# A third seven-product pair in the second half of an up-projection, with three small edits to the order around it

## The chip, the cores and the metric

The kernel runs on one core of a Trainium2 chip. The metric is device time in microseconds of one execution, as the median of the runs given; the profile is one execution of its own, with its own time. The engines are named as in the profile: PE is the matrix engine (PEld its weight loads), DVE the vector engine, ACT the scalar engine, POOL the GpSimd engine, SP the engine whose queue issues most transfers.

## The reference, cut to what matters

One layer of a streaming encoder on 512 positions of width 1024, all in float32. The part that the change touches is the last one, the channel mixer and what follows it:

```python
h = rms_norm(x, norm_ffn_g)
up = causal_dwconv(h @ w_up, conv_ffn_w)      # 1024 -> 2 x 2816, three taps over positions
a, b = jnp.split(up, 2, axis=-1)
x = x + (jax.nn.silu(a) * b) @ w_down         # 2816 -> 1024
return rms_norm(x, norm_f_g)
```

Before it stand a combined input projection, a short gated convolution, an attention with forget gates, and a gated merge of both; the change leaves them alone.

## The kernel before, in words

**Layout.** Features lie on the 128 partitions, the 512 positions in the free dimension. The 2816 hidden features are 22 pairs of blocks: pair `j` is the 128 columns of `a` (`up{2j}`) and the 128 of `b` (`up{2j+1}`).

**Precision.** Each float32 operand is split in a high part of a reduced type and the rest (`wh`, `wl` for weights, `x1h`, `x1l` and `gh`, `gl` for activations), and a product is three matmuls: high by high, rest by high, high by rest. A matmul is 128x128 weights by 256 positions. The split of a weight chunk is one ACT copy (line 275, writes `wh`) and one DVE subtraction (line 279, writes `wl`). `wh` and `wl` have two buffers each, so a chunk's `wh` can be written only when PE has done its last matmul with the `wh` of the chunk two before it, and likewise for `wl`.

**Plain and seven-product work.** A plain up block (`block`) multiplies eight weight blocks by two halves of the positions, three matmuls each: 48 matmuls, 96 a pair. A seven-product step (`seven`, a Strassen scheme) takes a 2x2 set of blocks and computes its eight products as seven. Its weights come in two chunks: `P`, three of the seven products with weights as they are, and `F`, four with sums of weights. A full step holds two such sets (a chunk `P` is 768 columns wide and gives 18 matmuls, a chunk `F` 1024 columns and 24), a half step one (9 and 12). A pair done in two full steps is 84 matmuls. Within a chunk the matmuls with `wh` come first (12 of 18, 16 of 24), those with `wl` after them. The sums of weights are made ahead of time in DRAM by `make_forms`: for each group of steps three transfers of SP and three accumulating transfers of POOL, put off to numbered slots. The sums of the activations are held in `gh` and `gl`: for the down projection six of the seven forms of a pair of pairs are in `go` and one in `ge`; for the up projection the forms of `x1` come through the tiles `y10` to `y13`, one after the other through one buffer: each is fetched from DRAM, split by ACT (`gh<-y`) and DVE (`gl<-y`), and only then is the next fetched.

**Order.** The hidden pairs are in two phases, 0 to 11 and 12 to 21. Each phase runs its up pairs (`up`) and then its part of the down projection as seven-product steps (`STEPS[0]`, `STEPS[1]`, through `seven`); the last products are plain (`dp` chunks). A step is named by its number: chunks `P30`, `F30` belong to step 30. A double like `((2, 6), (2, 7))` stands for outputs of set 2 and hidden pairs of pairs 6 and 7. Which up pairs are in seven products is in `SUP`.

**What the other engines do beside PE.** The result of an up block is multiplied by a row of norms (DVE, line 1171, `fz`), taken through the three taps (`taps`: ACT line 566, DVE lines 567 and 570, `fu`), gated (`glu`: ACT line 1231, POOL lines 1236 and 1243), and every second pair made into forms (DVE lines 1253 to 1258, then `hl` at lines 1262 and 1263). A pair in seven products has more to merge first (`merge`, lines 1192 to 1214). A list `later` holds such work; at each split of a chunk, `run_later` takes from its head what fits a budget in microseconds for that kind of chunk ("u" 1.7, "P" 1.6, "F" 0.75), and stops at a head that is due but too long. `flush` forces what the next matmuls need. Every engine then works through its own rows in the order in which the built program has them, and waits where a row's input isn't there.

**Banks.** PSUM has eight banks. A plain block takes the next in the list `acc`, a seven-product step a set of four: banks 2 to 5 for the pairs in `SUP[1]`, and the same four for set 2 at the end of phase 0, whose values are taken up by `combine` (lines 1282 to 1301).

Of the kernel before, what the change touches and what calls it, by code (L numbers as in the profile page):

```python
# [42 lines left out]
PHASES = ((0, 12), (12, NP))  # L43
# [4 lines left out]
STEPS = (  # L48
    tuple(((i, q), (i, q + 1)) for i, q in ((0, 0), (0, 2), (1, 0), (1, 2), (0, 4), (1, 4)))
    + tuple(((i, q), (i, q + 1)) for i in (3, 2) for q in (0, 2, 4)),  # L50
    (((2, 6), (2, 7)), ((2, 8), (2, 9)), ((0, 6), (0, 7)), ((0, 8), (2, 10)), ((0, 9), (0, 10)))
    + (((1, 6),), ((1, 7), (1, 8)), ((1, 9), (1, 10))),
)

# [3 lines left out]
PLAIN = [(m, k) for m in (6, 7) for k in range(*PHASES[1])]  # L58
PCUTS = (0, 8, 12, 20)

SUP = ((1, 2, 5), (14, 16))
XF = (26, 0)
UPD = tuple(tuple(((j, q), (j, q + 1)) for j in js for q in (0, 2)) for js in SUP)
DOUBLES = GATES + UPD[0] + STEPS[0] + UPD[1] + STEPS[1]
# [6 lines left out]
def block_kernel(ctx, tc, xT, vecs, wv, win, wmix, wo, wup, wst, wdp, outT):  # L71
# [84 lines left out]
    later = []  # L156
    held = dict.fromkeys(NRAW, 0)

    def after_split():

        st = ExitStack()
        for ins in order.values():
            st.enter_context(tc.issue_after(ins))
        return st
# [82 lines left out]
    def flush_only(tags):  # L247

        while n := [n for n, w in enumerate(later) if set(w[2]) & set(tags)]:
            with after_split():  # L250
                later.pop(n[0])[3]()
# [200 lines left out]
    for kb in range(KB):  # L452
        x = xs[kb]
# [236 lines left out]
    z, e, o = (ap.tile([n, S], F32, tag="pp", name=nm, bufs=NPP) for nm in ("fz", "fe", "fo"))  # L690
# [56 lines left out]
    acc, bank_s, bank_t = ring(2, 0, 1), ring(3, 4), ring(5, 6)  # L747
# [26 lines left out]
    for q in (0, 2):  # L774
        f, g = x_sums(slice(q, q + 2))
# [8 lines left out]
    for idx in late:  # L784
        kind, i = divmod(idx, 4)
# [338 lines left out]
    def turns(*ids):  # L1124
        st = list(ids)

        def f(name):
            f.last = st.pop(0)
            flush((f.last,))
            return bank(f.last, name)  # L1130

        return f
# [8 lines left out]
    def up(j, ph, rb2, pu=None):  # L1141
        uu = []

        def tap(i, z):
            u = fp.tile([P, S], F32, tag="fu", name=f"fu{j}{i}", bufs=3)
            taps(u, z, CF + 3 * (2 * j + i))
            uu.append(u)

        if j in SUP[ph]:
            c = 2 * SUP[ph].index(j)  # L1150
            slot()
            seven(
                UPD[ph][c : c + 2], NU[ph] + c, {j: USETS[j]}, lambda q, g: up_form(ph, q, g), of="x",
                done=lambda i, banks, ids: merge(ph, j, banks, ids, rb2, tap, uu),
            )
            slot()
            return
        evacs = []
        for i in range(2):
            slot()  # L1160
            p = pu[i] if pu else block(f"up{2 * j + i}", x1h, x1l, True)
            if i and j + 1 == PHASES[ph][1]:
                split_next()
                if any(("e",) in w[2] for w in later):
                    flush_only((("e",),))
                    split()
            z = [None]

            def mul(i=i, p=p, z=z):
                z[0] = fp.tile([P, S], F32, tag="fz", name=f"fz{j}{i}", bufs=4)  # L1170
                nc.vector.tensor_mul(z[0], p, rb2)

            evac = [(0.7, mul), (1.4, lambda i=i, z=z: tap(i, z[0]))]
            if i:
                evac.append((0, lambda: glu(ph, j, uu)))
            if any(("e",) in w[2] for w in later):
                later.extend((0, us, (("e",), acc.last) if x == 0 else (("e",),), f) for x, (us, f) in enumerate(evac))
            else:
                for _, f in evac:
                    f()  # L1180
# [46 lines left out]
    def glu(ph, j, uu):  # L1227
        a, b = uu
        q, k = j // 2, len(parts) - 1
        g0 = place(ph, q)  # L1230
        nc.scalar.activation(a, a, AF.Silu)
        if j == NP - 1:
            nc.scalar.activation(tbl, a[: 4 * H, :1], AF.Sqrt, scale=0.0, bias=eps[: 4 * H])
        if j % 2 == 0:
            ge = glu.even = fp.tile([P, 2, 2 * P], F32, tag="ge", name=f"ge{q}", bufs=2)
            keep(nc.gpsimd.tensor_mul(ge, a.rearrange(halves_of, h=2), b.rearrange(halves_of, h=2)))  # L1236
            return
        flush_only([("q", x) for x in range(q)])
        ge = glu.even
        go = fp.tile([P, 6, 2 * P], F32, tag="gr", name=f"go{q}")  # L1240

        def mul(eng):
            return eng.tensor_mul(go[:, 0:2, :], a.rearrange(halves_of, h=2), b.rearrange(halves_of, h=2))

        if j + 1 < PHASES[ph][1]:
            keep(mul(nc.gpsimd))
        else:
            later.append((k + 3, 0.7, (("q", q),), lambda: mul(nc.vector)))
        b11, b12 = ge[:, 0, :], ge[:, 1, :]
        b21, b22, t1, t2, t3, t4 = (go[:, i, :] for i in range(6))  # L1250

        def t13():
            nc.vector.tensor_sub(t1, b11, b12)
            nc.vector.tensor_sub(t3, b22, b12)

        def t24():
            nc.vector.scalar_tensor_tensor(t2, t1, -1.0, b22, op0=ALU.mult, op1=ALU.subtract)
            nc.vector.scalar_tensor_tensor(t4, t2, -1.0, b21, op0=ALU.mult, op1=ALU.subtract)

        def hl(src, gs):  # L1260
            def f():
                nc.scalar.activation(gh[:, gs, :], src, AF.Copy)
                nc.vector.tensor_sub(gl[:, gs, :], src, gh.bitcast(F32)[:, gs, :])

            return f


        d = (2, 3, 4) if j + 1 < PHASES[ph][1] else (4, 5, 6)
        w = [(d[0], 0.85, t13), (d[0], 0.85, t24), (d[1], 0.7, hl(ge[:, : 1 + ph, :], slice(g0, g0 + 1 + NF * ph, NF)))]
        w += [(d[x > 0 and 2 or 1], 0.7, hl(go[:, x : x + 2, :], slice(g0 + 1 + x, g0 + 3 + x))) for x in (0, 4, 2)]  # L1270
        at = next((x for x, i in enumerate(later) if ("e",) in i[2]), len(later))
        later[at:at] = [(k + n, us, (("q", q),), f) for n, us, f in w]

# [48 lines left out]
    X, Y = (6, 7, 0, 1), (2, 3, 4, 5)  # L1322
    for ph, (j0, j1) in enumerate(PHASES):
        if ph:
            acc = turns(*(6, 7, 0, 1) * 4)
            make_forms(ND[1], len(DOUBLES), ph)
        for j in range(j0, j1):
            pu = None
            if j == 0:
                nrm = {}  # L1330

                def mid():
                    nrm["c"] = rstd_col([ssq2], NT, 6, "n2")

                def late():
                    nrm["b"] = rstd_sb(rstd_bc(nrm["c"], NT, 7, "n2"), "n2")

                pu = lead(["up0", "up1"], x1h, x1l, mid, late)
            up(j, ph, nrm["b"], pu)
        if not ph:  # L1340
            up_forms(0, 1)
        flush_only((("e",),))
        seven(
            STEPS[ph], ND[ph], ({0: X, 1: Y, 3: X, 2: Y}, {0: X, 1: Y, 2: Y})[ph],
            lambda q, g: (gh[:, place(ph, q) + g, :], gl[:, place(ph, q) + g, :]),
            done=lambda i, banks, ids: combine(ph, i, banks, ids), tick=True,
        )
        assert not todo_bg
# [188 lines left out]
```

## Time and profile before

| | |
|---|---|
| median of 3 runs | 694.79 us (694.62 to 695.16) |
| the profiled execution | 694.18 us, its span 692.4 us |
| PE busy | 683.1 us, 99% of the span |
| DVE busy | 554.2 us, 80% |
| ACT busy | 368.3 us, 53% |
| POOL busy | 190.5 us, 28% |
| up pairs of phase 1 | 523.8 to 631.1 us in the span |
| down steps of phase 1 | 631.1 to 667.8 us |

PE's busy time counts matmuls that overlap in its pipeline as one stretch. In a timeline a row gives the start, the length, the engine, line and operation, and in brackets how long the engine had been idle and what ended that.

### The profile page before, as it was taken

The numbers are of one execution on the slowest core, as the hardware profiler recorded it, in microseconds if no ns is written. First come the engines' busy times: TensorE is split into PE (matmuls) and PEld (weight loads), VectorE is DVE, ScalarE is ACT, GpSimd is POOL, SyncE is SP. The second block draws the span as 40 slices with busy tenths as digits, with TensorE's granted clock in tenths as the row PEclk, the third lists the DMA queues.
The fourth block names the chain that finished last, engine by engine and source line by source line (L and its number), as shares of the span: only waits on it lengthen the run. The fifth ranks groups of instructions, "written<-read, shape, count | busy, mean of one in ns | idle before, by whom it ended". The sixth has DMA issues, their size and how long they took to land. (4 is left out here: it accounts for less than half of the span.)

```text
span 692.4 us, 14690 instructions
## 1 busy us (share of the span) xinstructions
PE 683.1 (99%) x5936; PEld 680.6 (98%) x5936; DVE 554.2 (80%) x858; ACT 368.3 (53%) x579; POOL 190.5 (28%) x201
## 2 busy tenths in 40 slices
PE   9999999999999999999999999999999999999996
PEld 9999999999999999999999999999999999999995
DVE  6677787877578778769879699998787899988894
ACT  5675755554554444546554555545444544545572
POOL 6134947542020201214400144340100325231000
PEclk9999999999999999999999999999999999999998
DMA  8629999552568586788998498888945996676413
GB/s 308 225 67 293 216 243 204 134 120 92 185 144 221 166 268 205 230 308 213 158 313 241 126 233 222 200 242 231 252 149 167 337 231 157 188 168 182 154 31 122
DMA packets 65012, 137.53 MB, mean 199 GB/s; under 512 B 5760, under 2 KB 30352, under 8 KB 64688
## 3 DMA queue, kind: packets, MB, share of 16 engines
q1 hardware_dynamic: 44664, 107.28, 47.2%
q0 software_dynamic: 18464, 26.03, 23.4%
q10 hardware_dynamic: 1816, 3.29, 1.3%
q8 instruction: 46, 0.75, 0.4%
q14 instruction: 22, 0.18, 0.1%
HBM read 132.31 MB, written 47.71 MB: 260 GB/s over the span
## 5 line engine op out<-in xcount | busy, mean ns | idle before, releaser
L211 POOL DMA_DIRECT2D f<-in_wst_dram x66 | 77.7, 1371 | 27.1 <-DMA f<-f 26.8
L309 PE MATMUL p_up<-x1h,wh_up 128*128 128x256 f32 x416 | 81.2, 276 | 0.0
L309 PE MATMUL p_up<-x1l,wh_up 128*128 128x256 f32 x416 | 81.0, 276 | 0.0
L309 PE MATMUL p_up<-x1h,wl_up 128*128 128x256 f32 x416 | 81.0, 276 | 0.0
L279 DVE TENSOR_TENSOR wl_F<-raw_F,wh_F 128x1024 fp32r<-128x1024 f32 (+1 forms) x42 | 55.9, 1330 | 20.0 <-ACT wh_F L275 20.0
L275 ACT ACTIVATE wh_F<-raw_F 128x1024 fp32r<-128x1024 f32 (+1 forms) x42 | 44.3, 1054 | 39.5 <-PE dn L327 28.7
L309 PEld LDWEIGHTS p_up<-x1h,wh_up 128*128 128x128 f32 x416 | 62.7, 188 | 0.0
L309 PEld LDWEIGHTS p_up<-x1l,wh_up 128*128 128x128 f32 x416 | 62.7, 188 | 0.0
L309 PEld LDWEIGHTS p_up<-x1h,wl_up 128*128 128x128 f32 x416 | 62.6, 188 | 0.0
L309 PE MATMUL p_in<-xgh,wh_in 128*128 128x256 f32 x288 | 56.8, 279 | 0.0
L309 PE MATMUL p_in<-xgh,wl_in 128*128 128x256 f32 x288 | 56.6, 278 | 0.0
L309 PE MATMUL p_in<-xgl,wh_in 128*128 128x256 f32 x288 | 56.5, 278 | 0.0
L279 DVE TENSOR_TENSOR wl_P<-raw_P,wh_P 128x768 fp32r<-128x768 f32 (+1 forms) x42 | 41.7, 992 | 14.7 <-ACT wh_P L275 8.6
L327 PE MATMUL dn<-gh,wh_F 128*128 128x256 f32 x216 | 51.2, 277 | 1.2 <-ACT wh_F L275 1.2
L275 ACT ACTIVATE wh_P<-raw_P 128x768 fp32r<-128x768 f32 (+1 forms) x42 | 35.1, 835 | 32.1 <-PE dn L327 23.2
L327 PE MATMUL dn<-gl,wh_F 128*128 128x256 f32 x216 | 51.0, 276 | 0.0
L1236 POOL TENSOR_TENSOR ge<-fu,fu 128x512 f32<-128x512 f32 x11 | 20.1, 1831 | 110.5 <-DVE fu L570 85.6
L279 DVE TENSOR_TENSOR wl_up<-raw_up,wh_up 128x1024 fp32r<-128x1024 f32 x34 | 43.8, 1288 | 7.4 <-ACT wh_up L275 7.4
L275 ACT ACTIVATE wh_up<-raw_up 128x1024 fp32r<-128x1024 f32 x34 | 35.8, 1054 | 19.4 <-PE p_up L309 9.3
L309 PEld LDWEIGHTS p_in<-xgh,wh_in 128*128 128x128 f32 x288 | 44.7, 188 | 0.7
L309 PEld LDWEIGHTS p_in<-xgl,wh_in 128*128 128x128 f32 x288 | 43.7, 188 | 0.0
L309 PEld LDWEIGHTS p_in<-xgh,wl_in 128*128 128x128 f32 x288 | 43.6, 188 | 0.0
(343 smaller groups left out, 2211.8 us busy)
## 6 DMA issues: line engine op xcount, KB each, us to landing
raw_F<-f SPq DMA_DIRECT2D x41, 512.0 KB, 5.7
raw_up<-in_wup_dram SPq DMA_DIRECT2D x34, 512.0 KB, 5.6
raw_P<-in_wst_dram SPq DMA_DIRECT2D x41, 384.0 KB, 5.4
raw_in<-in_win_dram SPq DMA_DIRECT2D x24, 512.0 KB, 3.6
f<-in_wst_dram POOLq DMA_DIRECT2D x41, 256.0 KB, 6.8
f<-in_wst_dram SPq DMA_DIRECT2D x20, 512.0 KB, 7.1
f<-in_wst_dram POOLq DMA_DIRECT2D x20, 512.0 KB, 9.1
f<-f SPq DMA_DIRECT2D x40, 256.0 KB, 6.5
```

Of the source, the lines that this page charges most:

```text
L211: return lambda: keep(nc.gpsimd.dma_start(dst, src, accum_op=ALU.add))
L275: ins = nc.scalar.activation(hi, raw, AF.Copy)
L279: ins = nc.vector.tensor_sub(lo, raw, hi.bitcast(F32))
L309: keep(nc.tensor.matmul(out[:, cs], w, x[:, cs], start=start and i == 0 and c == 0, stop=stop and i == 2 and c == len(cut) - 1,))
L327: keep(nc.tensor.matmul(out, wl if x == 1 else wh, xl if x == 2 else xh, start=opens and bk not in seen, stop=closes and bk not in left,))
L1236: keep(nc.gpsimd.tensor_mul(ge, a.rearrange(halves_of, h=2), b.rearrange(halves_of, h=2)))
```

## The change

```diff
-    (((2, 6), (2, 7)), ((2, 8), (2, 9)), ((0, 6), (0, 7)), ((0, 8), (2, 10)), ((0, 9), (0, 10)))
+    (((2, 6), (2, 7)), ((2, 8), (2, 9)), ((0, 6), (0, 7)), ((0, 8),), ((2, 10),), ((0, 9), (0, 10)))
     + (((1, 6),), ((1, 7), (1, 8)), ((1, 9), (1, 10))),
...
-SUP = ((1, 2, 5), (14, 16))
+SUP = ((1, 2, 5), (13, 15, 17))
...
             if i and j + 1 == PHASES[ph][1]:
                 split_next()
-                if any(("e",) in w[2] for w in later):
-                    flush_only((("e",),))
-                    split()
+                split()
+                flush_only((("e",),))
...
+            elif i and j + 1 == PHASES[ph][1]:
+                with after_split():
+                    for _, f in evac:
+                        f()
             else:
                 for _, f in evac:
                     f()
...
-        w += [(d[x > 0 and 2 or 1], 0.7, hl(go[:, x : x + 2, :], slice(g0 + 1 + x, g0 + 3 + x))) for x in (0, 4, 2)]
+        w.append((d[2], 1.7, hl(go, slice(g0 + 1, g0 + 7))))
...
-            acc = turns(*(6, 7, 0, 1) * 4)
+            acc = turns(*(6, 7, 0, 1) * 3, 6, 7)
```

**Pairs.** In phase 1 pairs 13, 15 and 17 are in seven products, where 14 and 16 were: three pairs for two. They use the same four banks 2 to 5 as before, the plain blocks the other four in turn. The steps of phase 1's down projection get higher numbers (36 to 44 for 34 to 41). The weight sums of the third pair, `f34`, are a third group, made in phase 0 behind the two that were there.

**A down step divided.** The step of `(0, 8)` and `(2, 10)` becomes two half steps, 39 and 40, with the same products; phase 1's down steps have six groups of weight sums where they had five.

**The six gated forms.** `go` was split into `gh` and `gl` in three pieces of 512 columns, two of them due a chunk apart, at 0.7 us each in the budget; now it is one piece of 1536 columns, due at the later time and 1.7 us in the budget.

**The last evacuation.** At the end of each phase the last up block's taps and gate stood right behind its matmuls; now both chunks of the first down step are split first.

What the built programs show of this at three places follows. The first is the start of phase 1, on DVE; `xm` there is the residual that `combine` adds set 2 of phase 0 to, from bank tile `dn1823`. Before:

```order
L279 TENSOR_TENSOR wl_up26_7050<-raw_up26_6808,wh_up26_7049 128x1024
L567 SCALAR_TENSOR_TENSOR fu120_6969<-fz120_6967,vec_64,fu120_6969 128x511
L1079 TENSOR_TENSOR gl_3989<-y13_6877,gh_3988 128x1024
L570 SCALAR_TENSOR_TENSOR fu120_6969<-fz120_6967,vec_64,fu120_6969 128x510
L1294 TENSOR_TENSOR xm_2605<-xm_2605,dn1823_6730 128x512
```

After, DVE again, at the same place:

```order
L279 TENSOR_TENSOR wl_P30_7034<-raw_P30_6791,wh_P30_7033 128x768
L567 SCALAR_TENSOR_TENSOR fu120_6957<-fz120_6955,vec_64,fu120_6957 128x511
L1079 TENSOR_TENSOR gl_3989<-y13_6864,gh_3988 128x1024
L570 SCALAR_TENSOR_TENSOR fu120_6957<-fz120_6955,vec_64,fu120_6957 128x510
L1297 TENSOR_TENSOR xm_2605<-xm_2605,dn1823_6712 128x512
```

The rows are the same but for the chunk; PE's chunk behind pair 12 was `up26`, a plain block in banks 0 and 1, and is now `P30`, whose fifth matmul writes the bank that held `dn1823`:

```order
L327 MATMUL dn30134_7041<-x1h_3990,wh_P30_7033 128x256
L327 MATMUL dn30134_7041<-x1l_3991,wh_P30_7033 128x256
L327 MATMUL dn30132_7039<-x1h_3990,wh_P30_7033 128x256
L327 MATMUL dn30132_7039<-x1l_3991,wh_P30_7033 128x256
L327 MATMUL dn30133_7040<-gh_3988,wh_P30_7033 128x256
```

The second place is the change from up to down in phase 1, on ACT. `fu210` and `fu211` are the last pair's taps, `tbl` the use of a newly loaded function table. Before:

```order
L275 ACTIVATE wh_P34_8267<-raw_P34_8063 128x768
L566 ACTIVATE fu210_8197<-fz210_8195,vec_64 128x512
L1231 ACTIVATE fu210_8197<-fu210_8197 128x512
L1233 ACT_TABLE_LOAD
L1233 ACTIVATE tbl_73<-fu210_8197,ex_87 32x1
L275 ACTIVATE wh_F34_8304<-raw_F34_8065 128x1024
L566 ACTIVATE fu211_8273<-fz211_8271,vec_64 128x512
L275 ACTIVATE wh_P35_8334<-raw_P35_8134 128x768
```

After:

```order
L275 ACTIVATE wh_P36_8242<-raw_P36_8023 128x768
L566 ACTIVATE fu210_8185<-fz210_8183,vec_64 128x512
L275 ACTIVATE wh_F36_8252<-raw_F36_8025 128x1024
L1265 ACTIVATE gh_3988<-ge9_7968 128x2x256
L1234 ACTIVATE fu210_8185<-fu210_8185 128x512
L1265 ACTIVATE gh_3988<-go9_8108 128x1536
L1236 ACT_TABLE_LOAD
L1236 ACTIVATE tbl_73<-fu210_8185,ex_87 32x1
L566 ACTIVATE fu211_8260<-fz211_8258,vec_64 128x512
L275 ACTIVATE wh_P37_8318<-raw_P37_8091 128x768
```

The gate and the table load moved from ahead of the first `F` chunk to ahead of the second `P` chunk, and the forms of `ge9` and `go9` stand there too. The same move at the end of phase 0 puts the gate of pair 11 (`fu110`) behind the first `F` chunk, without a table load.

The third place is the divided step, on ACT. Before:

```order
L1262 ACTIVATE gh_3988<-ge10_8131 128x2x256
L275 ACTIVATE wh_P37_8453<-raw_P37_8263 128x768
L1262 ACTIVATE gh_3988<-go10_8279 128x512 x3
L275 ACTIVATE wh_F37_8483<-raw_F37_8265 128x1024
L275 ACTIVATE wh_P38_8513<-raw_P38_8302 128x768
```

After:

```order
L275 ACTIVATE wh_P39_8433<-raw_P39_8238 128x384
L1265 ACTIVATE gh_3988<-ge10_8181 128x2x256
L275 ACTIVATE wh_F39_8452<-raw_F39_8240 128x512
L275 ACTIVATE wh_P40_8470<-raw_P40_8250 128x384
L1265 ACTIVATE gh_3988<-go10_8268 128x1536
L275 ACTIVATE wh_F40_8487<-raw_F40_8316 128x512
```

The forms `go10` stood behind the split of the chunk whose matmuls begin with `(0, 8)`; they now stand behind that of `P40`, the half step that begins with `(2, 10)` itself. DVE has the subtractions `gl` in the same places.

## The prediction

> **What bounds the kernel now.** I read the page first, then PE's waits, then PE's timeline where those waits fall, then the ACT and DVE rows around the three places that the change moves.
>
> ```profile
> span 692.4 us, 14690 instructions
> PE 683.1 (99%) x5936; PEld 680.6 (98%) x5936; DVE 554.2 (80%) x858; ACT 368.3 (53%) x579; POOL 190.5 (28%) x201
> PEclk9999999999999999999999999999999999999998
> ```
>
> PE is busy from end to end at full clock. So the time is PE's matmuls plus what PE waits, and a change is worth matmuls saved plus waits saved, less waits made. PE's waits in the part that changes:
>
> ```profile
> PE dn L327 <- ACT wh_F L275: 1.2, 2, 0.7
> PE dn L327 <- DVE wl_F L279: 0.4, 1, 0.4
> PE p_up L327 <- DVE wl_up L279: 0.2, 1, 0.2
> ```
>
> Four waits, all for a chunk's split. PE's timeline gives the matmul's pace and each wait's place:
>
> ```profile
> 320.00 0.39 PE L309 MATMUL p_wo<-ml,wh_wo 128*128 128x256 f32 x2
> ...
> 337.00 0.39 PE L309 MATMUL p_wo<-ml,wh_wo 128*128 128x256 f32 x2
> ...
> 468.62 0.38 PE L327 MATMUL dn<-gh,wh_F 128*128 128x256 f32 x1 [0.66 <-ACT wh_F L275]
> ...
> 535.16 0.28 PE L327 MATMUL p_up<-x1h,wh_up 128*128 128x256 f32 x1
> ...
> 554.09 0.28 PE L327 MATMUL dn<-gl,wh_F 128*128 128x256 f32 x1
> 554.72 0.38 PE L327 MATMUL dn<-x1h,wl_F 128*128 128x256 f32 x1 [0.35 <-DVE wl_F L279]
> 554.94 0.51 PE L327 MATMUL dn<-gh,wl_F 128*128 128x256 f32 x3
> ...
> 610.02 0.73 PE L327 MATMUL p_up<-x1h,wl_up 128*128 128x256 f32 x4 [0.15 <-DVE wl_up L279]
> ...
> 633.78 0.38 PE L327 MATMUL dn<-gh,wh_F 128*128 128x256 f32 x1 [0.50 <-ACT wh_F L275]
> ...
> 650.00 1.07 PE L327 MATMUL dn<-gh,wl_F 128*128 128x256 f32 x8
> ```
>
> From 320.00 to 337.00 are 75 such rows of two: 17.00/150 = 0.1133 us a matmul. That makes a plain block 5.44 us, a chunk P 2.04 (wh until 1.36), a chunk F 2.72 (wh until 1.81), halves of these in a half step. A wait costs more than its bracket: at 554.09 the next start was due at 554.20, came at 554.72, and the one behind it took 0.22 instead of 0.11, so 0.63 is lost for a bracket of 0.35. I take bracket plus 0.28 everywhere: 0.94, 0.63, 0.43 and 0.78, together 2.78 us.
>
> **The change, part by part.**
>
> *One more seven-product pair* removes 96 - 84 = 12 matmuls: 12 x 0.1133 = -1.36 us, all on the path. The third pair brings 3584 columns of splits where 2048 were, and a merge, to DVE, which has this room in the stretch of phase 1's up pairs:
>
> ```profile
> 523.80:631.10 107.30, 106.79 (x939) 106.40 (x938) 93.10 (x133) 53.19 (x74) 32.86 (x24) 1.00 0.78 215
> ```
>
> DVE (third busy time) has 14 us free of 107. The extra split is 1.23 x 1536/1024 = 1.8 us by the row of 1024 columns below, the merge some 2.7 us, so it fits on the whole; placing decides. Following DVE's new order row by row at the measured lengths, each wl lands 1 to 3 us before its use behind pair 13, also where 554.72 and 610.02 waited, since the forms' rows now stand elsewhere: -0.63 and -0.43. Were they to wait again, these return. The six more accumulating transfers of POOL and the three more groups of weight sums run beside this; they are due tens of microseconds before their chunk, and I cost them at nothing; if SP's queue, where later raw loads stand behind them, runs late, PE waits for raw weights, which no row of before shows.
>
> *Start of phase 1.* This is new. The rows of ACT and DVE:
>
> ```profile
> 533.00 1.06 ACT L1076 ACTIVATE gh<-y 128x1024 fp32r<-128x1024 f32 x1 [1.73 <-DMA y<-ys]
> 536.08 0.63 ACT L1231 ACTIVATE fu<-fu 128x512 f32<-128x512 f32 x1 [2.01 <-DVE fu L570]
> 536.62 1.05 ACT L275 ACTIVATE wh_up<-raw_up 128x1024 fp32r<-128x1024 f32 x1
> ...
> 534.10 1.23 DVE L1079 TENSOR_TENSOR gl<-y,gh 128x1024 fp32r<-128x1024 f32 x1 [1.46 <-ACT gh L1076]
> 535.24 0.74 DVE L570 SCALAR_TENSOR_TENSOR fu<-fz,vec,fu 128x510 f32<-128x510 f32 x1
> 535.90 0.68 DVE L1294 TENSOR_TENSOR xm<-xm,dn 128x512 f32<-128x512 f32 x1
> ...
> 541.36 1.76 DVE L279 TENSOR_TENSOR wl_P<-raw_P,wh_P 128x768 fp32r<-128x768 f32 x1
> ```
>
> The transfer of y13 lands at 533.00; behind it in DVE's queue stand gl, fu120 and line 1294, which empties its bank at 536.58. Before, nobody on PE needed that. Now the chunk in this place is P30, and its fifth matmul, due at 535.16, writes that bank: 536.58 + 0.05 - 535.16 = 1.47, and 0.11 for the restart: +1.6 us. (F30's wh, in the place of 536.62, is ready at 537.7, and F30 is due at 538.35 then; without the bank wait it would wait itself, 537.7 - 536.75 = 1.0.) P31's wl follows 0.6 us before 541.36, and in its 1.76 us, where such a row is 0.95 in quiet, ends at 542.5, about 0.1 after its use: +0.2. Together +1.8; bounds 1.0 and, if y13 lands 1 us later, 2.8.
>
> *The last evacuation.* In phase 0 F18's wh no longer stands behind the gate: it can start 0.20 after its buffer is free (650.00 against ACT's 650.20 below) and takes 1.05, while P18 takes 2.04: the wait at 468.62 goes, -0.94. P19's wh behind it has 3.4 us and is in time. In phase 1 the wait at 633.78 goes as well, -0.78, but what stood ahead of F is now ahead of the next P:
>
> ```profile
> 630.54 0.63 ACT L1231 ACTIVATE fu<-fu 128x512 f32<-128x512 f32 x1 [2.15 <-DVE fu L570]
> 631.19 1.28 ACT L1233 ACT_TABLE_LOAD   x1
> ...
> 632.69 1.04 ACT L275 ACTIVATE wh_F<-raw_F 128x1024 fp32r<-128x1024 f32 x1
> 633.64 0.71 ACT L566 ACTIVATE fu<-fz,vec 128x512 f32<-128x512 f32 x1
> 634.25 0.83 ACT L275 ACTIVATE wh_P<-raw_P 128x768 fp32r<-128x768 f32 x1
> ...
> 641.65 0.61 ACT L1262 ACTIVATE gh<-ge 128x512 fp32r<-128x512 f32 x1
> ...
> 650.20 1.07 ACT L275 ACTIVATE wh_F<-raw_F 128x1024 fp32r<-128x1024 f32 x1 [1.65 <-PE dn L327]
> ```
>
> Count from P36's first matmul. F36's wh begins at 0.20 and takes 1.04; then ge9 0.61, the gate 0.63, go9, the table with its first use 1.50 (631.19 to 632.69), fu211 0.71, P37's wh 0.83. No row has 1536 columns: from 512 (0.61) to 1024 (1.04) are 0.43, so 1.47; three pieces of 0.61 are the other end. The sum is 6.99, less four overlaps of 0.09 (632.69 + 1.04 against 633.64): 6.63. PE wants P37 at 2.04 + 2.72 = 4.76: 6.63 + 0.05 - 4.76 + 0.11 = +2.0 us, ends 1.9 and 2.4. [...]
>
> *The divided step.*
>
> ```profile
> 652.47 0.53 ACT L275 ACTIVATE wh_P<-raw_P 128x384 fp32r<-128x384 f32 x1 [0.94 <-PE dn L327]
> ...
> 642.92 0.69 DVE L1263 TENSOR_TENSOR gl<-ge,gh 128x512 fp32r<-128x512 f32 x1
> ...
> 633.76 1.23 DVE L279 TENSOR_TENSOR wl_F<-raw_F,wh_F 128x1024 fp32r<-128x1024 f32 x1 [1.79 <-ACT wh_F L275]
> ```
>
> The matmuls are as many as before. Count from P39's first: P39 1.02 (wh until 0.68), F39 1.36, so P40 is due at 2.38 and its fourth matmul, the first with gl of go10, at 2.72. ACT: P40's wh from 0.88, 0.53, to 1.41 (or 0.08 less); gh of go10 1.47, to 2.85. DVE: gl of 1536 columns is 1.23 + 0.54 = 1.77 by the two rows, to 4.65. So 4.65 + 0.05 - 2.72 + 0.11 = +2.1 us; with three pieces' lengths 2.4, and 1.9 if half the estimate is wrong. The half chunks' splits have 1.4 us or more against 0.53 and 0.64 and hide behind PE.
>
> *The six forms in one* at the other places: a saving of some 0.1 us of DVE each, off the path: 0. At P22, in phase 0, go5 is due to end 0.2 us before its first use: 0, bound +0.3.
>
> Sum: -1.36 - 2.78 + 1.8 + 2.0 + 2.1 = +1.8 us. The profiled execution is 694.18, the median of the runs 694.79, 0.6 above it; I add to the median: 696.6.
>
> **The rivals.**
>
> *More waits.* DVE is behind at one or two chunks behind pairs 13, 15, 17 as it was at 554.72 and 610.02: +0.63 and +0.43 are not saved, or the y chain is late by the third pair's raw loads that stand among its transfers (bound above): 697.6, up to 698.4. For it, DVE's load; against it, the slack that I find.
>
> *The y chain is early, and the change is not slower.* Its transfers:
>
> ```profile
> DMA to landing us min/median/max: 3.3/4.4/8.5
> ```
>
> If y12 and y13 both took the least, y13 would come about 1.2 us earlier, the bank would be free that much earlier and F30's wh as well: 1.8 - 1.2 = 0.6 of the new wait is left, 695.4. It decides from 0.4 us on. Against it: more bytes stand in the same queue now.
>
> *The clock falls.* The two waits of 2 us are longer than any before. At the end of the program PE is idle from 685.8:
>
> ```profile
> 685.80:686.20 0.40, 0.00 (x1) 0.00 (x0) 0.36 (x2) 0.00 (x0) 0.00 (x0) 1.00 0.00 0
> ...
> 687.40:687.80 0.40, 0.00 (x0) 0.00 (x0) 0.40 (x2) 0.00 (x0) 0.00 (x0) 0.74 0.29 95
> 687.80:688.20 0.40, 0.00 (x0) 0.00 (x0) 0.40 (x2) 0.00 (x0) 0.00 (x0) 0.50 1.02 366
> ```
>
> The granted clock goes from 1.00 to 0.50 about 1.8 us after the last matmul. In the waits at P37 and P40 PE is idle for 1.9 and 1.8. At half clock a matmul takes up to twice 0.1133; how long it would last no row shows: nothing, or the 4.6 us that it lasts to the span's end, half of it lost, 2.3 a wait. One such wait: 698.9. [...]
>
> **How the numbers follow.** 0.2% of the time, 1.4 us, is about what a measurement of this kernel can tell from no change; slower begins at 696.2. The likeliest case, three new waits at about my prices, has 0.50, own range 695.8 to 697.5; six tenths of it lie above 696.2. More waits 0.20, the clock 0.05, the early y chain 0.11; 0.14 is left for a gain that I don't see (the new waits hidden by something: at most -4.1, 690.7). Slower 0.30 + 0.20 + 0.05 = 0.55, within 0.2% 0.20 + 0.11 = 0.31, faster 0.14. The range is 694.5 to 698.9: its low end is the y chain early by the whole 1.8 and the other two waits at their lower ends (696.6 - 1.8 - 0.1 - 0.2), its high end the clock; below it only the unseen gain is left out.
>
> **What would show it.** In the changed profile PE's waits have three new rows: about 1.3 on DVE's line 1297 at P30, 1.8 on ACT's wh_P at P37, 1.7 on DVE's gl at P40; no wait for wh_F at F18 and F36; 5887 matmuls by the program for 5899. The granted clock stays at 1.00. I am wrong if P30's wait is short because y13 lands early, if ACT's long row is far from 1.47, or if PE waits at other up chunks.

## The result

The changed kernel takes 700.01 us (median of six, 697.38 to 702.41) where the kernel before, run beside it, takes 694.88: a ratio of 1.0068, interval 1.0049 to 1.0087. It is slower, by 5.1 us where 1.8 were forecast, and outside the range. A second comparison gave 699.32 against 695.35, ratio 1.0054 (1.0039 to 1.0070).

The six times are two groups: 697.38 to 698.59 at a mean granted clock of 0.997 or 0.998, and 701.43 to 702.41 at 0.993. The profiled execution, 698.36, is of the first group, 4.2 us above the one of before. Its page:

```profile
span 696.3 us, 14683 instructions
PE 682.4 (98%) x5924; PEld 679.9 (98%) x5924; DVE 558.7 (80%) x845; ACT 369.1 (53%) x562; POOL 196.8 (28%) x207
PEclk9999999999999999999999999999999999999998
```

12 matmuls fewer than before are on record (5924 for 5936), as forecast. PE's waits:

```profile
PE dn L327 <- ACT wh_P L275: 2.2, 1, 2.2
PE dn L327 <- DVE xm L1297: 1.6, 1, 1.6
PE p_up L327 <- DVE wl_up L279: 1.6, 1, 1.6
PE dn L327 <- DVE gl L1266: 1.4, 1, 1.4
```

The four waits of before (F18, F33, up41, F34) are gone. Four others stand in their place, and three of these are the forecast's: P37's on ACT's `wh_P`, P30's on DVE's line 1297, P40's on DVE's `gl`. The one on `wl_up` was not forecast. PE's timeline at the four places, the new one first:

```profile
445.23 0.28 PE L327 MATMUL p_up<-x1l,wh_up 128*128 128x256 f32 x1
447.06 0.74 PE L327 MATMUL p_up<-x1h,wl_up 128*128 128x256 f32 x4 [1.55 <-DVE wl_up L279]
...
536.44 0.28 PE L327 MATMUL dn<-x1l,wh_P 128*128 128x256 f32 x1
538.35 0.38 PE L327 MATMUL dn<-gh,wh_P 128*128 128x256 f32 x1 [1.63 <-DVE xm L1297]
...
639.10 0.39 PE L327 MATMUL dn<-gh,wh_P 128*128 128x256 f32 x1 [2.16 <-ACT wh_P L275]
...
653.37 0.39 PE L327 MATMUL dn<-gl,wh_P 128*128 128x256 f32 x1 [1.41 <-DVE gl L1266]
```

Taking 0.1133 us a matmul off the distance of starts, the place at 447.06 loses 2.1 us with its restarts (0.26 of it just ahead, at the chunk's start), P30 1.9, P37 2.6, P40 2.0. So -1.36 - 2.78 + 2.1 + 1.9 + 2.6 + 2.0 = +4.5, against 4.2 measured.

The wait at 447.06 is in phase 0, at the first block of pair 10 (`up20`), where nothing but the six forms was changed. DVE of before, ahead of that chunk's `wl_up` (the row of 2.00) and behind it:

```profile
442.04 0.69 DVE L1171 TENSOR_TENSOR fz<-p_up,rb_n 128x512 f32<-128x512 f32 x1
442.64 2.00 DVE L279 TENSOR_TENSOR wl_up<-raw_up,wh_up 128x1024 fp32r<-128x1024 f32 x1
444.57 0.41 DVE L1253 TENSOR_TENSOR go<-ge 128x256 f32<-128x256 f32 x1
```

And after:

```profile
439.09 0.41 DVE L1256 TENSOR_TENSOR go<-ge 128x256 f32<-128x256 f32 x1
...
441.74 0.68 DVE L1170 TENSOR_TENSOR fz<-p_up,rb_n 128x512 f32<-128x512 f32 x1
442.34 1.20 DVE L1266 TENSOR_TENSOR gl<-ge,gh 128x256 fp32r<-128x256 f32 x1
443.47 1.75 DVE L1266 TENSOR_TENSOR gl<-go,gh 128x1536 fp32r<-128x1536 f32 x1
445.14 0.74 DVE L567 SCALAR_TENSOR_TENSOR fu<-fz,vec,fu 128x511 f32<-128x511 f32 x1
445.80 1.21 DVE L279 TENSOR_TENSOR wl_up<-raw_up,wh_up 128x1024 fp32r<-128x1024 f32 x1
```

The forms of the pair of pairs before, with the one piece of 1536 columns, came behind the chunk's split and now stand ahead of it. Over these rows DVE has no gap in either kernel, so the split ends at 447.01 where it ended at 444.64.

### The profile page after: what moved, and what is told of

Its sections match the earlier page's. It is cut to its first block, busy times and chain, and to the rows that moved or that the text cites. A ratio compares the mean times of both kernels' runs of the same rounds, so it can differ in the third digit from the quotient of the medians.

```text
span 696.3 us, 14683 instructions
## 1 busy us (share of the span) xinstructions
PE 682.4 (98%) x5924; PEld 679.9 (98%) x5924; DVE 558.7 (80%) x845; ACT 369.1 (53%) x562; POOL 196.8 (28%) x207
## 4 chain that ended last, share of the span: by engine, by line
PE 86%; DVE 9%; DMA 2%; ACT 1%; issue 1%; DVEq 0%; ACTq 0%
PE dn L327 28%; PE p_in L309 14%; PE p_up L309 12%; PE p_wo L309 6%; PE p_up L327 3%; PE yc L309 3%; PE ya L309 3%; DVE wl_up L279 2%; PE pa L477 2%; DMA y<-ys 2%; PE pb L479 2%; PE p_q L309 2%; PE p_k L309 2%; PE o L658 2%; DVE fu L570 1%; DVE fu L567 1%
## 5 line engine op out<-in xcount | busy, mean ns | idle before, releaser
L211 POOL DMA_DIRECT2D f<-in_wst_dram x72 | 83.5, 1412 | 27.4 <-DMA f<-f 27.1
L309 PE MATMUL p_up<-x1l,wh_up 128*128 128x256 f32 x392 | 76.4, 276 | 0.0
L309 PE MATMUL p_up<-x1h,wh_up 128*128 128x256 f32 x392 | 76.4, 276 | 0.0
L309 PE MATMUL p_up<-x1h,wl_up 128*128 128x256 f32 x392 | 76.3, 276 | 0.0
L309 PEld LDWEIGHTS p_up<-x1l,wh_up 128*128 128x128 f32 x392 | 59.1, 188 | 0.0
L309 PEld LDWEIGHTS p_up<-x1h,wh_up 128*128 128x128 f32 x392 | 59.0, 188 | 0.0
L309 PEld LDWEIGHTS p_up<-x1h,wl_up 128*128 128x128 f32 x392 | 59.0, 188 | 0.0
L279 DVE TENSOR_TENSOR wl_P<-raw_P,wh_P 128x768 fp32r<-128x768 f32 (+1 forms) x45 | 44.4, 986 | 14.0 <-ACT wh_P L275 8.0
L327 PE MATMUL dn<-gh,wh_F 128*128 128x256 f32 x228 | 53.9, 276 | 0.0
L327 PE MATMUL dn<-gl,wh_F 128*128 128x256 f32 x228 | 53.9, 276 | 0.0
```

Of the source, the lines that this page charges most:

```text
L211: return lambda: keep(nc.gpsimd.dma_start(dst, src, accum_op=ALU.add))
L279: ins = nc.vector.tensor_sub(lo, raw, hi.bitcast(F32))
L309: keep(nc.tensor.matmul(out[:, cs], w, x[:, cs], start=start and i == 0 and c == 0, stop=stop and i == 2 and c == len(cut) - 1,))
L327: keep(nc.tensor.matmul(out, wl if x == 1 else wh, xl if x == 2 else xh, start=opens and bk not in seen, stop=closes and bk not in left,))
```

## The experiments

Ahead of the channel mixer, where nothing is changed, the profiles differ by up to 2.6 us. Where profiles are compared I therefore take the mixer's own length, from PE's first `pb_n` matmul near 349 to the start of its last row of them: 349.19 to 685.19, 336.0 us, before; 349.34 to 689.64, 340.3, after.

**The two groups.** The changed kernel, unaltered, three times.

> The changed kernel once more, unaltered. In six executions it took 697.4 to 698.6 us three times, at a mean granted clock of 0.997 to 0.998, and 701.4 to 702.4 three times, at 0.993; one of the first kind is profiled. Theory (a wait of PE that lasts about 2 us lets the clock fall, the one at P37 with 2.16 us above all): again two groups some 4 us apart, the longer with the clock of 0.993; should a longer execution be profiled, the granted clock is 0.5 for some microseconds behind P37's wait and 1.0 elsewhere. Rival (the clock's fall has nothing to do with PE's waits): one group only on this chip, or a fall at another place.

Measured: three executions of 697.25 to 698.68, three of 699.96 to 700.25 at 0.995 or 0.996. The profile was again of the shorter group, with the same waits (P30's was 0.9).

> The changed kernel, unaltered, for a profile of its longer group. Theory: if the mean clock is 0.995 or 0.993, the granted clock is at 0.50 once or twice for 3.4 us, beginning in or just behind the waits at P37 (2.1) or P40 (1.4), or at P30. Rival: at another place.

> The changed kernel, unaltered, once more, in case the first look falls in the shorter group; the expectations are those of the first look.

Both of these are of the longer kind: 700.62 us at a clock of 0.995, 701.82 at 0.992. In the first the clock falls once, at P37; in the second twice. Windows of half a microsecond of the second (the seventh value from the left, behind POOL's count, is the granted clock):

```profile
538.00:538.50 0.50, 0.00 (x0) 0.00 (x0) 0.50 (x2) 0.50 (x1) 0.00 (x0) 1.00 1.01 326
538.50:539.00 0.50, 0.45 (x3) 0.45 (x4) 0.50 (x1) 0.50 (x2) 0.00 (x0) 0.90 0.91 309
539.00:539.50 0.50, 0.50 (x4) 0.50 (x3) 0.50 (x2) 0.50 (x1) 0.00 (x0) 0.50 1.02 334
...
542.00:542.50 0.50, 0.50 (x5) 0.50 (x4) 0.50 (x2) 0.00 (x0) 0.00 (x0) 0.69 0.74 301
542.50:543.00 0.50, 0.50 (x6) 0.50 (x5) 0.50 (x2) 0.00 (x0) 0.07 (x1) 1.00 0.46 188
...
641.00:641.50 0.50, 0.50 (x4) 0.50 (x5) 0.50 (x2) 0.50 (x1) 0.00 (x0) 0.80 0.00 0
...
644.50:645.00 0.50, 0.50 (x5) 0.50 (x5) 0.07 (x1) 0.00 (x0) 0.00 (x0) 0.79 0.83 123
```

A window with 0.90 was at 1.0 for four fifths and at 0.5 for one. So the clock was down from 538.90 to 542.31, right behind P30's wait, and from 641.30 to 644.71, right behind P37's: 3.41 us each time. Within the first, PE's matmuls start 0.21 us apart (five from 539.10 to 540.16) where 0.1133 is the pace; by the clock of 0.50 I put its cost at 1.7 us, half of 3.41. From the end of the first to the start of the second are 98.99 us, 29.0 times 3.41: both falls of this execution lie on one grid of stretches of that length. The rival, a fall elsewhere, is out for these two executions.

**How long a wait it takes.** The kernel before, with one of its splits written several times over (same values):

```diff
-            ins = nc.scalar.activation(hi, raw, AF.Copy)
+            for _ in range(4 if nm == "F20" else 0):
+                nc.scalar.activation(hi, raw, AF.Copy)
+            ins = nc.scalar.activation(hi, raw, AF.Copy)
```

> The kernel before, with ACT writing wh of F20 four times more ahead of the one write (the same values; 0.97 us each), so that PE has one wait of about 2.3 us at F20 in a stretch where it waits for nothing else. It costs 2.5 us where the clock holds. Theory (the clock is set in stretches of 3.4 us that don't follow the program, and halves for the next 3.4 us when PE was idle for 1.8 or more of one): a wait of 2.3 lies with 1.8 or more in one stretch in (3.4 - 1.8 + 2.3 - 1.8)/3.4 = 0.6 of the executions, which take another 3.4/2 = 1.7 us: two groups, 2.5 and 4.2 us over the kernel before, with clocks of 0.997 and 0.994. Rival (the clock falls only after 3.4 us without a matmul): one group at 2.5 us.

The built order put other ACT rows between the writes, so the wait came out at 3.54, not 2.3, and the costs expected for 2.3 don't apply:

```profile
482.11 0.46 PE L329 MATMUL dn<-gh,wh_F 128*128 128x256 f32 x1 [3.54 <-ACT wh_F L277]
```

699.86 us against 694.99, ratio 1.0070 (1.0057 to 1.0084). Of five executions one held the clock (698.21, 0.997); four were at 0.995 or 0.993, 1.5 to 3.2 longer. With a wait of 3.54, a stretch of 3.41 without a matmul fits in only 0.13/3.41 = 4% of executions, so the rival is hardly possible.

> The kernel before with wh of F20 written two times more (four times more gave a wait of 3.5 us, and the lower clock in four of five executions). The wait is 3.54 - 2 x 0.97 = 1.6 us, which costs 1.8. Theory (1.8 or more of a stretch of 3.4 us must be idle): the clock never falls, 1.8 us over the kernel before, all in one group. Rival (any wait over 1 us can do it): some executions another 1.7 us longer, clock 0.994.

The wait was only 0.40 by the same reshuffling, so this run says nothing on 1.6: no execution of twelve had a clock below 0.996.

> The kernel before with wh of F20 written three times more. By ACT's order the wait at F20 is that of four times more (3.54) less one write and one piece of the forms, 1.04 + 0.51: 2.0 us. Theory (1.8 or more of a stretch of 3.4 idle): the lower clock in about half of the executions, which are 1.7 us longer, the rest 2.1 us over the kernel before at 0.997. Rival (a whole stretch of 3.4 us idle): never; all in one group.

```profile
480.44 0.38 PE L329 MATMUL dn<-gh,wh_F 128*128 128x256 f32 x1 [2.07 <-ACT wh_F L277]
```

Here the wait is as worked out. Four of six executions are 696.53 to 697.48 at 0.997, two 698.58 and 698.89 at 0.995; before beside them 695.00. By their mean clock, with a lone wait of 2.07 the clock fell in two of six executions, which the rival, a whole stretch of 3.4 idle, excludes.

The profiles fix my bound of 1.8 more closely. The last fall of each, behind its last matmul, lies a whole number of stretches behind the one in the mixer (640.75 and 695.36 in the first longer profile: 16.0 times 3.413). So I lay the stretches back from it, also where the clock held, which takes them to run on there too; they cut a wait in two. First the stretch ahead of the fall at 538.90, then the one with the longer of P37's waits in the run with three pieces and y13 later (below), which held the clock, then the two that share the wait of 2.07 above (PE's busy time is the second value):

```profile
535.49:538.90 3.41, 1.62 (x15) 1.43 (x13) 2.88 (x4) 1.40 (x3) 0.00 (x0) 1.00 0.99 337
635.37:638.78 3.41, 1.66 (x14) 1.57 (x14) 3.41 (x5) 1.96 (x3) 0.00 (x0) 1.00 0.13 35
475.55:478.96 3.41, 2.82 (x25) 2.62 (x24) 0.69 (x2) 3.35 (x4) 0.00 (x0) 1.00 0.70 215
478.96:482.37 3.41, 1.93 (x17) 1.93 (x18) 1.95 (x3) 2.78 (x5) 0.00 (x0) 1.00 0.00 0
```

PE was idle for 1.79 in the first, and the clock fell at its end; for 1.75, 0.59 and 1.48 in the others, and it held. In the mixers of all profiles here, the eight stretches with a fall behind them have 1.79 to 3.25 of idle, all others at most 1.75. So in these mixers the idle time within one stretch tells the falls from the rest, and by it the same wait goes with a fall or not by where the stretches lie. At the end of the program a fall came with 1.17 in one profile, so the figure is one for the mixers alone. Two things stay open, as no profile has them: the execution above that held the clock at a wait of 3.54, and the four at 0.994 of the kernel below that waits for `go10` in the whole step, whose profiled execution held it with 1.52 in a stretch.

**The six forms.** The one piece back in three:

```diff
-        w.append((d[2], 1.7, hl(go, slice(g0 + 1, g0 + 7))))
+        w += [(d[x > 0 and 2 or 1], 0.7, hl(go[:, x : x + 2, :], slice(g0 + 1 + x, g0 + 3 + x))) for x in (0, 4, 2)]
```

> The changed kernel with the six gated forms in three pieces again, due as before. Theory: the one piece of 1536 columns is what makes up10's second chunk wait in phase 0 (1.55 on DVE's wl, 2.1 us lost), and its being longer than a budget also shifted the gate and the table load of pair 21 ahead of P37's split. So the wait in phase 0 is gone, P37's shrinks from 2.16 to 0.5 or less, P40's from 1.41 to about 0.4, P30's stays at 1.6: 698.4 - 2.1 - 2.2 - 1.3 = about 692.8 us for the profiled execution, 693.4 as median, all executions within 1 us of each other, clock 0.997. Rival (DVE is behind in phase 0 because the third group of weight sums makes POOL and DVE slow each other): the wait of 1.55 stays, some 695.

694.80 us against 695.35, ratio 0.9995 (0.9981 to 1.0009); at a clock of 0.997 it takes 693.0 to 694.8. PE's waits:

```profile
PE dn L327 <- DVE wl_P L279: 1.7, 1, 1.7
PE dn L327 <- DVE xm L1297: 1.3, 1, 1.3
PE dn L327 <- DVE gl L1266: 0.7, 1, 0.7
```

(The expectations' second chunk of up10 is `up20`, the first block of pair 10.) The waits at `up20` and at P40 are gone: the first as the theory had it, the second wholly where 0.4 was expected to stay. P37's did not shrink; the 0.7 and the 1.7 are both P37's, now on DVE. That part of the expectation missed, and in the profile the clock falls right behind them, where both share a stretch with 2.25 of idle (5 of 12 executions are at 0.995 or less).

The other way round, the kernel before with the one piece alone:

> The kernel before with the six gated forms in one piece of 1536 columns, nothing else. Theory (this edit alone makes the second chunk of up10 wait in phase 0, by the order that it gives DVE, not by the third group of weight sums): a wait of 1.5 on DVE's wl_up there, +2.1 us; the step of (0, 8) and (2, 10) waits for go10 as well, 0.5 to 1.5: 697.5 to 698.5 against 695 of before. Rival (the wait needs the third pair's transfers): no wait in phase 0, 695 to 696.

697.00 us against 694.93, ratio 1.0030 (1.0021 to 1.0040). The wait at `up20` is there with 1.59, so it needs neither the third pair nor its weight sums. F18's wait is gone here too, and F34's grew from 0.50 to 1.1, so the 2.1 of the times is not this wait alone. No wait came in the step of (0, 8) and (2, 10), where 0.5 to 1.5 was expected: one piece is late there only if DVE is late already.

**The third pair alone**, on the kernel before:

```diff
-SUP = ((1, 2, 5), (14, 16))
+SUP = ((1, 2, 5), (13, 15, 17))
...
-            acc = turns(*(6, 7, 0, 1) * 4)
+            acc = turns(*(6, 7, 0, 1) * 3, 6, 7)
```

> The kernel before with the third seven-product pair alone (pairs 13, 15, 17 for 14, 16), the other three edits not made. 12 matmuls less, -1.36; F18's wait (0.94) and F36's (about 0.8) stay as before; P30's bank wait comes, +1.5; the waits at 554.72 and 610.02 go, -1.06. Theory (the wait at P37 comes from the last evacuation that was moved behind F36's split, on DVE as on ACT): no wait at P37, so 0.9 under the kernel before, between -1.5 and 0. Rival (DVE is behind there because pair 17's merge comes late): P37 waits 1 to 2.5 us here too, and the kernel is 0.5 to 1.5 us slower than before.

699.94 us, ratio 1.0085 (1.0071 to 1.0100): as slow as the whole change, though it has 12 matmuls fewer than before. The rival is right, and its price too low: without the one fall of the clock in the profile the mixer takes 339.4 us, 3.4 more than before. (The executions at 0.998 are as long as the profiled one at 0.995, which stays open.) DVE of before at the same place, from the first row of the forms `go9` to the split of the first down chunk:

```profile
614.14 0.42 DVE L1253 TENSOR_TENSOR go<-ge 128x256 f32<-128x256 f32 x1
...
626.35 0.68 DVE L1263 TENSOR_TENSOR gl<-go,gh 128x512 fp32r<-128x512 f32 x1
...
627.55 1.45 DVE L279 TENSOR_TENSOR wl_P<-raw_P,wh_P 128x768 fp32r<-128x768 f32 x1
```

And with the third pair, DVE from the split of P36 on, and in a second block PE's wait for F36's `wh`:

```profile
627.97 1.75 DVE L279 TENSOR_TENSOR wl_P<-raw_P,wh_P 128x768 fp32r<-128x768 f32 x1
629.64 0.41 DVE L1253 TENSOR_TENSOR go<-ge 128x256 f32<-128x256 f32 x1
...
639.36 1.28 DVE L1263 TENSOR_TENSOR gl<-go,gh 128x512 fp32r<-128x512 f32 x2
```

```profile
635.71 0.39 PE L327 MATMUL dn<-gh,wh_F 128*128 128x256 f32 x1 [2.96 <-ACT wh_F L275]
```

Before, the forms `go9` were complete before the first down split; with pair 17 in seven products they are begun behind it, 15 us later (629.64 for 614.14), and the last pair's taps, its gate and the table load come later with them. That is what the change from up to down pays for. Whether it is the third pair's work or pair 17's late place, no run separates. With the order of before the wait stands at F36 (2.96), and in the step of (0, 8) and (2, 10) there is one of 1.36 for `gl` of `go10`; in the changed kernel, which splits F36 early, the first stands at P37.

**The table load** of pair 21's gate, put off by five chunks:

```diff
-            nc.scalar.activation(tbl, a[: 4 * H, :1], AF.Sqrt, scale=0.0, bias=eps[: 4 * H])
+            later.append((k + 5, 0, (), lambda: nc.scalar.activation(
+                tbl, a[: 4 * H, :1], AF.Sqrt, scale=0.0, bias=eps[: 4 * H]
+            )))
```

> The changed kernel with the table load and its first use put off by some chunks, to behind wh of P39; fu211 is then behind P37's wh too. P37's wait loses the load (1.5 us) and fu211 (0.6): from 2.16 it goes to about 0.3; the other three waits stay (1.55, 1.63, 1.41), unless the load now makes P40's forms later by up to 1.5. 698.4 - 2.1 = 696.3 us, up to 697.8. Theory on the clock: with the longest wait under 2 us no execution is of the longer kind, all within 1 us, clock 0.997 or 0.998. Rival: half of the executions still show 0.993 and take 4 us longer, so it is not P37's wait.

699.43 us, ratio 1.0056 (1.0039 to 1.0072), as slow as the changed kernel. P37 loses 2.3 us, where it lost 2.6, now 0.4 on DVE's `gl`, 0.9 on DVE's `wl_P` and the rest in restarts and short gaps (of the 1.9 below, 1.4 are P40's):

```profile
PE dn L327 <- DVE gl L1268: 1.9, 2, 1.4
PE dn L327 <- DVE wl_P L279: 0.9, 1, 0.9
```

So at P37 DVE stands right behind ACT. On the clock the run is inconclusive: its times spread over 3.3 us at clocks of 0.996 to 0.998, which the one profile does not explain; this stays open.

**The divided step** made whole again in the changed kernel:

```diff
-    (((2, 6), (2, 7)), ((2, 8), (2, 9)), ((0, 6), (0, 7)), ((0, 8),), ((2, 10),), ((0, 9), (0, 10)))
+    (((2, 6), (2, 7)), ((2, 8), (2, 9)), ((0, 6), (0, 7)), ((0, 8), (2, 10)), ((0, 9), (0, 10)))
```

> The changed kernel with the step of (0, 8) and (2, 10) whole again. Theory: P40's wait for gl of go10 (1.41, 2.0 us lost with its restarts) goes, since the forms are wanted only in F39 then; the three other waits stay: 696.4 us for the shorter executions, and as P37's wait of 2.16 stays, the longer kind (some 700, clock 0.993) is still there. Rival: the forms of 1536 columns are late for the whole step too, and a wait of 1 to 2 us stands at F39: 697.4 to 698.4.

703.20 us, ratio 1.0105 (1.0088 to 1.0122): worse, beyond the rival's price. In the whole step PE waits 0.72 for `gh` and 1.41 for `gl`, 2.7 us lost with the restarts, where the two half steps lose 2.0:

```profile
PE dn L327 <- DVE gl L1266: 1.4, 1, 1.4
PE dn L327 <- ACT gh L1265: 0.7, 1, 0.7
```

The rest of the distance is not the step's. The profiled execution is 2.3 us late before the mixer begins (351.65 for 349.34): PE's first matmuls go at about half the pace until 10.34 there, until 6.34 in the changed kernel (0.21 us a matmul from 5.50 to 6.34, 0.12 from there to 8.24), which the granted clock doesn't show: it is 1.00 there in the changed kernel from the start. And all five executions are at 0.992 to 0.994; the profile has one fall, behind P37's wait. The mixer, without that fall, takes 341.2 us for the changed kernel's 340.3. So the divided step is no cost of this change but takes some of it away.

**y13 later**, first alone in the changed kernel, then with the three pieces:

```diff
-            due = [c[0] for c in stream].index(f"F{ND[0] + len(STEPS[0]) - 2}") + q
+            due = [c[0] for c in stream].index(f"F{ND[0] + len(STEPS[0]) - 2}") + q + 3 * (q == 3)
```

> The changed kernel with the split of y13 one chunk later, nothing else. Theory (P30's wait is the bank behind y13 in DVE's queue): P30's wait (0.9 to 1.6, with restart 1.1 to 2.0) goes, no other comes in its place, the three other waits stay: 1.1 to 2.0 us less than the changed kernel's shorter group of 697.3 to 698.6, that is about 696.3; a longer group 2 to 4 us above it stays. Rival (F30's wh takes its place): 697.3 or more.

698.54 us. P30's wait is gone and none came in its place:

```profile
PE dn L327 <- ACT wh_P L275: 2.1, 1, 2.1
PE p_up L327 <- DVE wl_up L279: 1.6, 1, 1.6
PE dn L327 <- DVE gl L1266: 1.4, 1, 1.4
```

Four of the five executions had the clock fall (0.995), 697.88 to 699.37, so the median shows little. The mixer takes 340.1 us with one fall of 1.7, that is 338.4 without, 1.9 less than the changed kernel. The 696.3 expected of an execution without a fall was not seen; the one at 0.997 took 698.59.

> The changed kernel with the six forms in three pieces, and the split of y13 one chunk later (behind the split of F30, where it stood behind that of P30; it is first wanted in P31). Theory (P30 waits because line 1297, which empties its bank, stands in DVE's queue behind y13): P30's wait, 1.32 in the run with three pieces alone, is gone and no other takes its place, as F30's wh is then free of the gate that stood behind y13 too; 1.5 us less than that kernel, 691.5 to 692.3 where the clock doesn't fall. P37's two waits on DVE (0.68 and 1.75) stay, and the clock falls there in some executions. Rival (F30's wh or P31's gl is late in its place): 1.0 us of it comes back, 692.5 to 693.3.

693.95 us against 694.99, ratio 0.9986 (0.9977 to 0.9995). The two executions at 0.997 take 692.29 and 692.85, the upper end of what was expected; P37's waits are unchanged (0.7 and 1.7), and 9 of 11 are at 0.994 or 0.995; the profile is not one of these, so the place of their falls is not shown.

**P37's waits.** Built on that, in phase 1:

```diff
             elif i and j + 1 == PHASES[ph][1]:
-                with after_split():
-                    for _, f in evac:
-                        f()
+                if ph:
+                    flush_only([("q", x) for x in range(j // 2)])
+                    later.insert(0, (len(parts), 0, (acc.last,), lambda e=tuple(evac): [f() for _, f in e]))
+                else:
+                    with after_split():
+                        for _, f in evac:
+                            f()
...
-            later.append((k + 3, 0.7, (("q", q),), lambda: mul(nc.vector)))
+            later.append((k + 2, 0.7, (("q", q),), lambda: mul(nc.vector)))
...
-        d = (2, 3, 4) if j + 1 < PHASES[ph][1] else (4, 5, 6)
+        d = (2, 3, 4) if j + 1 < PHASES[ph][1] else (3, 4, 5)
```

> Built on the kernel with three pieces and y13 later (692.3 to 692.9 us undisturbed, 693.95 as median): in phase 1 the last up block's taps and gate are put behind the split of P37, not of F36 (the forms of go9 are forced ahead of it), and what hangs on them is due one chunk earlier, counted from there. Theory (P37's two waits, 0.68 and 1.75, 2.9 us lost, are DVE's queue: two taps and a row of norms, 3.3 us, stand between wl of F36 and wl of P37): both waits go, 1.4 us of idle and half clock with them; 689.5 us, all executions within 1 us, clock 0.997. Rival (DVE is behind in this stretch as a whole, so that moving rows only moves the wait): a wait of 1.5 to 3 us comes at P38 or at P40 for go10, 691 to 693.

690.64 us against 694.93: ratio 0.9941, interval 0.9925 to 0.9956. No execution of six is below a clock of 0.997. From its page, and then what is left of PE's waits in the mixer:

```profile
span 688.5 us, 14722 instructions
PE 680.3 (99%) x5924; PEld 678.7 (99%) x5924; DVE 560.8 (81%) x867; ACT 370.3 (54%) x584; POOL 192.5 (28%) x207
```

```profile
PE dn L327 <- DVE wl_P L279: 0.8, 1, 0.8
```

The mixer takes 332.8 us, 3.2 less than before: 1.36 of matmuls and 2.78 of old waits, less P37's 1.2, and some short gaps fewer. The theory holds for 1.9 of the waits' 3.1 us (its 2.9); the last part of P37's wait stays, behind the forms of `go9`. Nothing new came at P38 or P40. This kernel is faster than both.

> The kernel of the first run of this call with the step of (0, 8) and (2, 10) whole again. Theory (the divided step gives go10 1.7 us more, since (2, 10) begins 2.38 us behind the step's first matmul, not 0.68): whole, it waits for go10, 0.5 to 1.7 us more than with the divided one, where go10 is in time or nearly so. Rival (the divided step costs time by itself, as its small chunks leave ACT and DVE less room): it is the faster of the two by up to 1 us.

694.04 us, 3.4 more than with the step divided. PE waits 0.2 for `gh` and 1.36 for `gl` of `go10`, 2.2 lost, and four of twelve executions are at 0.994.

**The last evacuation in phase 0 alone**, on the kernel before: the first weights of the down projection are split first there, as in the change, and phase 1 is as it was.

```diff
-                if any(("e",) in w[2] for w in later):
+                if not ph:
+                    split()
+                    flush_only((("e",),))
+                elif any(("e",) in w[2] for w in later):
                     flush_only((("e",),))
                     split()
...
+            elif i and j + 1 == PHASES[0][1]:
+                with after_split():
+                    for _, f in evac:
+                        f()
             else:
```

> The kernel before with the last evacuation behind the first down weights at the end of phase 0 alone. F18's wait for wh (0.66, 0.94 us lost) goes and nothing else changes: 0.9 us less than the kernel before. Rival (the gate of pair 11 that now stands behind F18's split makes P19 wait): no change.

694.50 us against 694.99, ratio 0.9994 (0.9985 to 1.0003). F18's wait is gone, no wait at P19 came, and the wait at `up41` grew from 0.15 to 0.44. What is left of 0.9 can't be told from nothing by the times.

## Why the prediction was wrong

| step of the prediction | forecast, us | measured |
|---|---|---|
| 12 matmuls fewer | -1.36 | 12 fewer on record |
| F18, F33, up41, F34 | -2.78 | all four waits gone |
| P30 and P31 | +1.8 | +1.9, P31 nothing |
| P37 | +2.0 | +2.6 |
| P40 | +2.1 | +2.0 |
| the six forms elsewhere | 0, bound +0.3 | +2.1 at `up20` |
| the clock | 0, a rival at 0.05 | 0, +1.7 or +3.4, in 8 of 14 executions not 0 |

*The step that failed* is "The six gated forms in one at the other places". I priced the rows (a tenth of a microsecond of DVE saved) and looked at P22, where the chunk is a seven-product one, not at `up20`, where DVE of the changed kernel has no gap from 439 to 447 and the order had moved four form rows, the small `gl` and the large one ahead of `wl_up`. Both the one piece alone and its undoing show it: 1.59 with it, nothing without.

*The clock* was a rival with far too small a chance: 0.05, where the clock fell in 8 of 14 executions. Its price was 2.3 a fall, where 3.41 us at a clock of 0.50 is measured, some 1.7, and of its places P37 was right; the other fall that a profile shows is behind P30's wait, none behind P40's. The 0.05 was my estimate, which no run bears out: the trace's own row, where the clock fell 1.8 us behind the last matmul, spoke for more. The falls make the distance from 698.4 to the median. The executions without one lie inside the range, but by luck: its high end was set by a fall, and what filled it was the wait at `up20`.

*The three new waits* were where the prediction put them. P37's was 0.6 larger: ACT waited 0.39 for DVE's forms of `go9` there, a row that my sum had as ready:

```profile
634.60 1.49 ACT L1265 ACTIVATE gh<-go 128x1536 fp32r<-128x1536 f32 x1 [0.39 <-DVE go L1261]
```

But the causes that it names are only half right. P37's wait is not the evacuation's move alone: with the order of before it stands at F36 with 2.96, because the forms of `go9` come later with pair 17 in seven products and DVE is late by it. My "it fits on the whole" took DVE's 14 us of 107 for room at the end, where there was none (12.93 us busy of the 13 from 628 to 641 in the changed kernel). P40's wait is not the divided step's: it comes of the one piece and of that lateness, and the division shortens it.

*P30* is as forecast, mechanism and size: the bank's last reader stood behind y13, and moving y13 took the wait away. Its size varied from 0.9 to 1.9 over four profiles of the same kernel, by when y13 landed and when PE came to P30 (y13's `gl` begins at 535.81 and 535.86 in two of them, P30 at 536.10 and 536.87, with waits of 1.63 and 0.91). F30's wait of 1.0, which I expected behind it, did not come: with y13 moved, ACT begins F30's `wh` at 536.68, where it began at 538.33.

## What to carry to other kernels

On an engine whose rows follow without a gap, an edit that moves rows is priced by the due time of whatever now stands behind them, at each place where it does so, also where the edit was not meant to act. Extra work costs where it is done, so a saving that is bought with work on the second engine should not be placed last before a change of stage. And a wait of PE of about 2 us can cost more than its length: one of 2.07 us went with a lower clock in two of six executions, 1.1 to 2.4 us longer than the rest. In the mixers of the profiles the clock fell behind each stretch of 3.41 us with 1.79 us or more of idle, so by my estimate several short waits are cheaper than one long one, as long as they don't stand within the same stretch.

## What the runs showed of the hardware

The changed kernel's profiled executions have no, one or two falls of the clock in the mixer; the two of the second longer profile show as a granted clock of 0.50 for 3.41 us each, some 1.7 us lost by my estimate, with 29.0 such stretches between them, and in the first longer profile the fall behind the last matmul starts 16.0 stretches after the one in the mixer. By the mean clock, a lone wait of 2.07 us was enough in two of six executions, one of 3.54 in four of five; in the profiles it fell behind each stretch with 1.79 us of idle or more and behind none with 1.75 or less in the mixer. In the changed kernel's mixer an ACT copy of 1536 columns took 1.47 to 1.50 us and the DVE subtraction of it 1.74 to 1.76, as the estimates from 512 and 1024 columns had them (1.47 and 1.77).
